# Stores to intermediate DRAM buffers issued by GpSimd in place of SyncE, in a two-layer encoder kernel

## The chip, the core and the metric

The kernel runs on one core of a Trainium2 chip. A core has TensorE (matmul, PE in the profile; PEld is its weight load), VectorE (DVE), ScalarE (ACT), GpSimd (POOL) and SyncE (SP). Each engine works through its own list of instructions in order and waits for the others on semaphores. A DMA is issued by an engine (SP, ScalarE or GpSimd) from its list, and 16 DMA engines move the bytes. The metric is the device time of one execution in microseconds (us).

## The reference

Two layers work on x of 2048 tokens with 1024 features, float32.

```python
def even_layer(x, ...):
    h = rmsnorm(x, norm_pre)
    xa, za, xb, gb, gc, zb = split(h @ w_in)               # 1024 x 6144
    ua = centred_dwconv(xa, conv_w, 2) + conv_b
    ya = rg_lru(ua, ..., False) + rg_lru(ua, ..., True)    # scans over the tokens, both ways
    ya = ya * silu(za)
    yb = gb * centred_dwconv(gc * xb, sc_w, 1) * silu(zb)
    return x + rmsnorm(concat([ya, yb]) @ w_out, norm_post)

def odd_layer(x, ...):
    h = rmsnorm(x, norm_pre)
    q, k, v, r, lr = split(h @ w_in)                       # 512, 512, 1024, 1024, 32
    log_alpha = log_sigmoid(lr @ w_gate_lr + b_gate) / 16  # one for each direction
    o = gla(q, k, v, log_alpha[0]) + flip(gla(flip(q, k, v, log_alpha[1])))
    o = rmsnorm(o, head_norm_g)                            # per head, 4 heads
    return x + rmsnorm((o * silu(r)) @ w_out, norm_post)
```

## The kernel before

All matrices are held as pairs of float16 (a high and a low part), and a product is three matmuls: high x high, high x low, low x high. The large products use a scheme of seven block products in place of eight (`quad`, `seven`, `wq_seven`), so each operand and each weight exists as seven sums or differences of blocks. These do not all fit on the chip. They are written to buffers in DRAM and read back when their block comes. The buffers, as the profile names them:

- hd, written from H by `op_save` (line 580): the seven operands of the even layer's input product, for two halves of the tokens x; read back by `op_loader` 107 times (H<-hd).
- yd, from YH by `yfin` (962): the 16 rows of blocks of the even mixer's result; read back as YC.
- x (x1 in the source), from XR by `post_even` (1249): the even layer's result.
- gd, from H by `op2_save` (1306): the seven operands of the odd layer; read back 56 times (H<-gd).
- wdqk, wdv, wdr, from hl by `save_u` in `w_prep` (1399): the odd layer's weights in seven sums for q and k, v, r; wzd the small gate weight. wqd, from PC and hl by `save_q` (1442): the odd layer's output weights.
- vd, rd, gld, yod: v (`v_save`), the gate r (`r_out`), the decays (`decays`) and the odd mixer's result (`y_out`).

The kernel is written as some fifty Python generators ("threads"), each for one strand of the work. The class `Order` runs them at build time. Each step of a thread announces an engine and an estimated cost, and the planner picks the step that can start first by its own clock. The instruction is put into its engine's list at that moment. On the chip each engine follows its list in order. A DMA counts as engine "D" in the plan: `dma` (line 282) announces bytes / 360e3 us and issues on SP. So SP's list holds loads and stores mixed, in the order of the plan, and an instruction of SP that waits holds up all behind it: a store waits until its data are computed, a load until its buffer is free.

Buffers on the chip come from pools: 23 large slots with a limit for each role (H, YL, H2, ...), the weight slots raw (3 or more), and hl, which during `w_prep` serves as small pieces. `w_prep` runs while TensorE does the even layer's output product (lines 1176 to 1178, `wo_mm`). For each pair of weight blocks, `prep` (1449) takes a piece for a running sum, makes seven results (high part on ScalarE, line 255; low part on VectorE, line 259; sums on VectorE, line 263) and stores each one; a piece is given back after its store (`pput`). In the same time `post_even` evacuates the product, normalises it and makes the odd layer's operands; the sum over features is a product with ones, split in two parts (`ones_mm2`, hv, line 463).

A wdv buffer has 256 columns, and each store fills 128 of them:

```python
def save(j, p):
    d = wu_d[u, j]
    yield from dma(d[:, :, :, i * 128:i * 128 + 128] if u[0] == "v" else d, p.t, 256 * 1024)
    pput(p)
```

GpSimd's own work before the change is two masks at the start (`consts`) and two memsets in `wz_load` (lines 1508 and 1509), which wait for the end of the even layer's output product.

Of the kernel before, what the change touches and what calls it, by code (L numbers as in the profile page):

```python
# [8 lines left out]
F16 = mybir.dt.float16  # L9
# [153 lines left out]
def trunk_kernel(ctx: ExitStack, tc: tile.TileContext, xT, w_in, gate_w, w_out, odd_w, lr_w, lr_gw, odd_wo, params, outT):  # L163
    nc = tc.nc
# [114 lines left out]
        yield from stt(out, v, 3.0 / scale, out, ALU.subtract, ALU.mult)  # L279
        unbank(b)  # L280

    def dma(out, in_, nbytes):
        yield ("D", nbytes / 360e3)
        nc.sync.dma_start(out=out, in_=in_)

    def done(ev):
        ev.t = S.cur.ready
# [287 lines left out]
    OPS = {}  # L575
    evOp = {}
    h_d = [[drams.tile([128, 4, 2, CH], F16, tag=f"h{x}{j}", name=f"hd{x}{j}") for j in range(7)] for x in range(2)]
    evHd = [[Ev() for _ in range(7)] for _ in range(2)]

    def op_save(x, j):  # L580
        yield ("w", evOp[x, j])
        yield from dma(h_d[x][j], OPS[x, j].t, 2 ** 20)
        done(evHd[x][j])
        if x == 0:
            if j in (0, 2, 4):
                yield ("w", ev_plain)
            put(OPS[x, j])
# [370 lines left out]
    y_d = [drams.tile([128, 2, T], F16, tag=f"y{i}", name=f"yd{i}") for i in range(16)]  # L958
# [3 lines left out]
    def yfin(ki, y):  # L962
        yh = yield from get("YH", [128, T])
        yield from act(yh.t, y.t, AF.Square, accum=ssq[:, ki:ki + 1])
        yield ("V", 0.35)
        e = sex[:, ki:ki + 1]
        nc.vector.tensor_scalar(out=e, in0=ssq[:, ki:ki + 1].bitcast(I32), scalar1=24, scalar2=None,
                                op0=ALU.arith_shift_right)
        nc.vector.tensor_scalar(out=sY[:, ki:ki + 1], in0=e, scalar1=-1, scalar2=202, op0=ALU.mult, op1=ALU.add)
        nc.vector.tensor_scalar(out=sW[:, ki:ki + 1], in0=e, scalar1=1, scalar2=65, op0=ALU.mult, op1=ALU.add)  # L970
        nc.vector.tensor_scalar(out=sY[:, ki:ki + 1], in0=sY[:, ki:ki + 1], scalar1=23, scalar2=None,
                                op0=ALU.arith_shift_left)
        nc.vector.tensor_scalar(out=sW[:, ki:ki + 1], in0=sW[:, ki:ki + 1], scalar1=23, scalar2=None,
                                op0=ALU.arith_shift_left)
        done(evS[ki])
        yv = yh.t.bitcast(F16)
        hi, lo = yv[:, 0:T], yv[:, T:2 * T]
        yield from act(hi, y.t, AF.Copy, scale=sYf[:, ki:ki + 1])
        yield from stt(lo, y.t, sYf[:, ki:ki + 1], hi, ALU.mult, ALU.subtract)
        put(y)  # L980
        yield from dma(y_d[ki].rearrange("p a t -> p (a t)"), yv, 2 ** 20)
        put(yh)
        done(evY[ki])

# [233 lines left out]
    x1_d = [[drams.tile([128, 4, CH], F32, tag=f"x1{c}{h}", name=f"x1{c}{h}") for h in range(2)] for c in range(NCH)]  # L1218
# [30 lines left out]
    def post_even():  # L1249
        yield ("w", ev_proj)  # L1250
        for c in range(NCH):
            if c == 0:
                yb = []
                for _ in range(2):
                    s = yield from get("YB", [128, 4, CH])
                    yb.append(s)
            tmp = yield from wget("hv", [128, 2, CH], F32)
            yield from evac_norm({m: _LazyOB(OB, c, m) for m in range(8)}, [evO[c, m] for m in range(8)], yb, tmp, 1, 2.0 ** -13, gsc[:, 0:8])
            b = yield from ones_mm2("fg", tmp.t[:, 0], late=4.0 if c < 3 else 0.0)
            r = tmp.t[:, 1]  # L1260
            yield from rsq(r, b, 1.0 / 1024, 0)
            for hf in range(2):
                yield ("w", evXR[c, hf])
                x, y = XR[c, hf].t, yb[hf].t
                yield from tt(y, y, r[:, None, :].to_broadcast([128, 4, CH]), ALU.mult)
                yield from tt(x, x, y, ALU.add)
                yield from act(y, x, AF.Square)
                yield from dma(x1_d[c][hf], x, 2 ** 20)
                if hf:
                    done(evX1[c])  # L1270
            yield from tt(yb[0].t, yb[0].t, yb[1].t, ALU.add)
            y = yb[0].t
            yield from tt(y[:, 0:2], y[:, 0:2], y[:, 2:4], ALU.add)
            yield from tt(y[:, 0], y[:, 0], y[:, 1], ALU.add)
            b = yield from ones_mm2("fg", y[:, 0], late=4.0 if c < 3 else 0.0)
            yield from rsq(r, b, 1.0 / (1024 * 4096), 1)
            if c == NCH - 1:
                for s in yb:
                    put(s)
            for hf in range(2):  # L1280
                x = XR[c, hf].t
                for k in range(4):
                    yield from stt(x[:, k], x[:, k], gsc[:, 16 + hf * 4 + k:17 + hf * 4 + k], r, ALU.mult, ALU.mult)
                if c % 2 == 0:
                    S.spawn(op2_make(c // 2, 2 * hf, XR[c, hf]), 1)
            if c % 2:
                S.spawn(op2_rest(c // 2), 1)
            wput(tmp)
            done(evH2[c])

    class _LazyOB:
# [3 lines left out]
        t = property(lambda s: s.d[s.k].t)  # L1295
# [5 lines left out]
    OP2 = {}  # L1301
    evOp2 = {(x, j): Ev() for x in range(2) for j in range(7)}
    h2_d = [[drams.tile([128, 4, 2, CH], F16, tag=f"g{x}{j}", name=f"gd{x}{j}") for j in range(7)] for x in range(2)]
    evH2d = [[Ev() for _ in range(7)] for _ in range(2)]

    def op2_save(x, j):
        yield from dma(h2_d[x][j], OP2[x, j].t, 2 ** 20)
        done(evH2d[x][j])

    def op2_make(x, j, src):  # L1310
# [58 lines left out]
    wq_d = [drams.tile([128, 4, 2, 512], F16, tag=f"wq{j}", name=f"wqd{j}") for j in range(8)]  # L1369
# [25 lines left out]
    wz_d = drams.tile([128, 2, 512], F16, tag="wzd", name="wzd")  # L1395
# [3 lines left out]
    def w_prep():  # L1399
        yield ("w", ev_proj)  # L1400
        w = W["lr", 0]
        yield ("w", w.evr)
        for hf in range(2):
            p = yield from pget()
            LRP.append(p)
            src = w.raw.t[:, hf * 4:hf * 4 + 4]
            yield from act(p.t[:, 0], src, AF.Copy, scale=1024.0)

            lo = p.t[:, 1, :, 96:128]
            yield from stt(lo, src[:, :, 96:128], 1024.0, p.t[:, 0, :, 96:128], ALU.mult, ALU.subtract)  # L1410
            yield from act(p.t[:, 0, :, 96:128], lo, AF.Copy)
        wput(w.raw)
        done(evLRP)
        def save_u(u, i, last):
            def save(j, p):
                d = wu_d[u, j]
                yield from dma(d[:, :, :, i * 128:i * 128 + 128] if u[0] == "v" else d, p.t, 256 * 1024)
                pput(p)
                if last:
                    done(evWD[u, j])  # L1420
            return save

        for u in UNITS:
            prs = ukeys(u)
            for i, pr in enumerate(prs):
                yield from prep(W[pr[0]], W[pr[1]], save_u(u, i, i == len(prs) - 1))
            if u == UNITS[0]:
                w = W["wz", 0]
                p = yield from pget()
                wz = p.t.rearrange("p a k m -> p a (k m)")  # L1430
                yield ("w", w.evr)
                raw = w.raw.t.rearrange("p k m -> p (k m)").rearrange("p (d n) -> p d n", d=2)
                yield from act(wz, raw, AF.Copy, scale=256.0)
                yield from stt(wz[32:64], raw[32:64], 256.0, wz[32:64], ALU.mult, ALU.subtract)
                wput(w.raw)
                yield from dma(wz_d, wz, 256 * 1024)
                pput(p)
                done(evWZd)

        done(evPrep)  # L1440

    def save_q(hd):
        def save(j, p):
            yield from dma(wq_d[j][:, hd], p.t.rearrange("p a k m -> p a (k m)"), 256 * 1024)
            pput(p)
            count(("wq", j), 4, lambda: done(evWQd[j]))
        return save
# [192 lines left out]
    V = [[None, None] for _ in range(4)]  # L1640
    evVd = [Ev() for _ in range(4)]
    v_d = [[drams.tile([128, 8, 256], F32, tag=f"v{h}{x}", name=f"vd{h}{x}") for x in range(2)] for h in range(4)]
# [17 lines left out]
                         wfin, ofin)  # L1660

    def v_save(h, x):
        yield from dma(v_d[h][x], V[h][x].t, 2 ** 20)
        put(V[h][x])
        done(evVs[h][x])

# [26 lines left out]

    def r_out(h, x, s):
        yield from act(s.t, s.t, AF.Silu)
        yield from dma(r_d[h][x], s.t.rearrange("p a i t -> p a (i t)"), 2 ** 20)
        put(s)
        done(evRd[h][x])

# [68 lines left out]
    def decays(d):  # L1768
# [4 lines left out]
        for hd in range(4):  # L1773
# [35 lines left out]
                rng = crt[:, 1:16]  # L1809
            put(t1)  # L1810
            yield from act(rng, rng, AF.Exp, scale=-1.0 / 16)
            yield from dma(g_d[hd, d], t2.t, 2 ** 20)
            put(t2)
            done(evGd[hd, d])
        count("decays", 2, lambda: put(LMS[0]))
# [235 lines left out]

    def y_out(hd, c, yl):
        n = yn(c)
        yield from dma(yo_d[hd][c][:, 0:n], yl.t.bitcast(F16)[:, 0:n], 256 * n)
        put(yl)
        done(evYO[hd, c])

# [367 lines left out]
```

## Time and profile before

| | |
|---|---|
| median of 3 runs | 2169.05 us (2167.36 to 2171.09) |
| the profiled execution | 2169.87 us, its span 2168.0 us |
| TensorE busy | 2128.0 us (98%) |
| VectorE, ScalarE busy | 1579.9 us (73%), 1266.2 us (58%) |
| GpSimd busy | 2.8 us, 8 instructions |
| DMA | 458.36 MB, mean 211 GB/s; queue q1 took 57.2% of the 16 engines' span |
| granted TensorE clock | 0.997 |

The span runs from the first to the last instruction of the profiled execution. In rows of the timeline the first two numbers are the start and the duration in us, then the engine, the line of the source, the operation, what it writes and reads (by the program's names, numbers left out), the shape, and in brackets how long the engine stood idle before it and what ended the wait. SPq is SP's queue: a row there is the issue of a DMA, not its transfer. Rows of waits give who waited, for whom, and the total, the number of times and the longest in us. Rows of DMA issues end with the median time from issue to landing. Rows of stretches give for each engine its busy time, then the granted clock, the busy share of the DMA engines and GB/s.

### The profile page before, as it was taken

To read this page: it belongs to the slowest core of one execution; us is meant where nothing else is said; L and a number is where in the kernel's file an instruction comes from. 1 tells how busy PE (TensorE), PEld (TensorE's weight loads), DVE (VectorE), ACT (ScalarE), POOL (GpSimd) and SP (SyncE) were. 2 spreads that over 40 slices of the span, in tenths; PEclk is the share of its full clock that TensorE was granted. 3 is DMA by queue.
4 is the path that set the end of the run, shared out by engine and by line. 5 is a ranking of instruction groups with operands and counts; after the bars stand their busy time and mean duration, and the time that the engine had idled before them with its cause. 6 is when DMAs were issued, how large, how long until landed. Compare 5 with 4: busy or idle time off the path is not lost.

```text
span 2168.0 us, 28942 instructions
## 1 busy us (share of the span) xinstructions
PE 2128.0 (98%) x11650; PEld 1196.4 (55%) x11650; DVE 1579.9 (73%) x1908; ACT 1266.2 (58%) x1701; POOL 2.8 (0%) x8
## 2 busy tenths in 40 slices
PE   8999999999999999999999999999999999999997
PEld 5444444444444444444444444777657484858886
DVE  6998878887879787867467875676535748485866
ACT  5466877768677667765434443366446556466522
POOL 0000000000000000000000000000000000000000
PEclk9999999999999999999999999999999999999999
DMA  7165444555736555549767684147672939576353
GB/s 263 64 252 224 153 182 162 211 195 190 261 137 221 221 190 211 197 152 341 241 190 241 233 293 184 77 170 297 248 291 103 358 124 349 199 301 270 141 189 133
DMA packets 146150, 458.36 MB, mean 211 GB/s; under 512 B 39776, under 2 KB 60384, under 8 KB 111840
## 3 DMA queue, kind: packets, MB, share of 16 engines
q1 hardware_dynamic: 146016, 456.52, 57.2%
q8 instruction: 91, 1.49, 0.3%
q14 instruction: 43, 0.35, 0.1%
HBM read 329.99 MB, written 126.48 MB: 211 GB/s over the span
## 4 chain that ended last, share of the span: by engine, by line
PE 82%; DVE 8%; DMA 5%; ACT 3%; issue 2%; SPq 1%; ACTq 0%; DVEq 0%
PE ps L840 16%; PE ps L842 16%; PE ps L841 15%; PE ps L1178 3%; PE ps L1176 3%; PE ps L1177 3%; PE ps L1919 2%; PE ps L2154 2%; PE ps L2155 2%; PE ps L2156 2%; PE ps L1584 2%; PE ps L1586 2%; PE ps L1585 2%; PE ps L926 2%; PE ps L1887 1%
## 5 line engine op out<-in xcount | busy, mean ns | idle before, releaser
L840 PE MATMUL ps<-H,hl 128*128 128x512 f16 x848 | 322.3, 380 | 6.2 <-ACT QS L255 3.0
L841 PE MATMUL ps<-H,hl 128*128 128x512 f16 x848 | 322.1, 380 | 0.7 <-DVE H L263 0.7
L842 PE MATMUL ps<-H,hl 128*128 128x512 f16 x848 | 322.0, 380 | 0.2
L842 PE MATMUL ps<-H,PC 128*128 128x512 f16 x728 | 275.9, 379 | 1.0 <-DVE PC L259 1.0
L840 PE MATMUL ps<-H,PC 128*128 128x512 f16 x728 | 275.9, 379 | 0.8 <-DMA H<-hd 0.8
L841 PE MATMUL ps<-H,PC 128*128 128x512 f16 x728 | 275.9, 379 | 0.0
L1178 PE MATMUL ps<-YC,WO 128*128 128x512 f16 x512 | 194.1, 379 | 0.3 <-DVE WO L259 0.3
L1176 PE MATMUL ps<-YC,WO 128*128 128x512 f16 x512 | 194.1, 379 | 0.0
L1177 PE MATMUL ps<-YC,WO 128*128 128x512 f16 x512 | 194.0, 379 | 0.0
L840 PEld LDWEIGHTS <-hl 128*128 128x128 f16 x848 | 83.1, 98 | 103.9 <-issue 3.1
L842 PEld LDWEIGHTS <-hl 128*128 128x128 f16 x848 | 83.1, 98 | 102.3 <-issue 1.9
L841 PEld LDWEIGHTS <-hl 128*128 128x128 f16 x848 | 83.2, 98 | 101.4 <-issue 4.8
L1584 PE MATMUL ps<-WV,H 128*128 128x256 f16 x448 | 122.1, 273 | 1.8 <-ACT VD L255 1.8
L1585 PE MATMUL ps<-WV,H 128*128 128x256 f16 x448 | 122.1, 273 | 0.0
L1586 PE MATMUL ps<-WV,H 128*128 128x256 f16 x448 | 122.1, 273 | 0.0
L255 ACT ACTIVATE hl<-raw 128x512 f16<-128x512 f32 (+1 forms) x129 | 80.0, 629 | 69.2 <-DMA wdv<-hl 16.6
L842 PEld LDWEIGHTS <-PC 128*128 128x128 f16 x728 | 71.2, 98 | 87.2 <-DVE PC L259 1.5
L840 PEld LDWEIGHTS <-PC 128*128 128x128 f16 x728 | 71.2, 98 | 87.1 <-DMA H<-hd 1.3
L841 PEld LDWEIGHTS <-PC 128*128 128x128 f16 x728 | 71.2, 98 | 86.0 <-issue 0.3
L259 DVE SCALAR_TENSOR_TENSOR hl<-raw,hl 128x512 f16<-128x512 f32 (+2 forms) x129 | 87.4, 685 | 42.8 <-ACT hl L255 42.6
L155 ACT ACT_TABLE_LOAD x86 | 110.3, 1283 | 1.5
L263 DVE TENSOR_TENSOR SB<-ps,SB 128x256 f32<-128x256 f32 x112 | 46.4, 423 | 79.7 <-PE ps L1919 78.1
(252 smaller groups left out, 4523.2 us busy)
## 6 DMA issues: line engine op xcount, KB each, us to landing
H<-hd SPq DMA_DIRECT2D x107, 1024.0 KB, 6.2
H<-gd SPq DMA_DIRECT2D x56, 1024.0 KB, 10.3
raw<-w_in SPq DMA_DIRECT2D x48, 512.0 KB, 4.3
yd<-YH SPq DMA_DIRECT2D x16, 1024.0 KB, 4.9
YC<-yd SPq DMA_DIRECT2D x64, 256.0 KB, 5.0
hd<-H SPq DMA_DIRECT2D x14, 1024.0 KB, 4.8
gd<-H SPq DMA_DIRECT2D x14, 1024.0 KB, 4.2
raw<-odd_w SPq DMA_DIRECT2D x24, 512.0 KB, 5.6
```

Of the source, the lines that this page charges most:

```text
L155: self.load(SETS[self.table][0])
L255: nc.scalar.activation(out=out, in_=in_, func=func, scale=scale, **kw)
L259: nc.vector.scalar_tensor_tensor(out=out, in0=in0, scalar=scalar, in1=in1, op0=op0, op1=op1)
L840: nc.tensor.matmul(b.t[:, sl], lhsT=wh, rhs=hi, start=s, stop=False, skip_group_check=True)
L841: nc.tensor.matmul(b.t[:, sl], lhsT=wh, rhs=lo, start=False, stop=False, skip_group_check=True)
L842: nc.tensor.matmul(b.t[:, sl], lhsT=wl, rhs=hi, start=False, stop=e, skip_group_check=True)
L1176: nc.tensor.matmul(b.t, lhsT=wh, rhs=hi, start=start, stop=False)
L1177: nc.tensor.matmul(b.t, lhsT=wh, rhs=lo, start=False, stop=False)
L1178: nc.tensor.matmul(b.t, lhsT=wl, rhs=hi, start=False, stop=stop)
L1584: nc.tensor.matmul(b.t[:, i], lhsT=hi, rhs=wh, start=st, stop=False, skip_group_check=True)
L1585: nc.tensor.matmul(b.t[:, i], lhsT=hi, rhs=wl, start=False, stop=False, skip_group_check=True)
L1586: nc.tensor.matmul(b.t[:, i], lhsT=lo, rhs=wh, start=False, stop=e, skip_group_check=True)
```

## The change

The helper for DMAs gets an argument for the issuing engine, and 13 stores of the source pass GpSimd: all that write an intermediate buffer. In the program 203 of SP's 696 instructions move to GpSimd's list: 14 hd, 16 yd, 8 x, 14 gd, 84 wdqk, wdv and wdr, 1 wzd, 32 wqd, 6 vd, 8 rd, 8 gld and 12 yod. The loads and the ten stores of the output stay on SP. The announced cost in the plan is unchanged, and so the lists of TensorE, VectorE and ScalarE hold the same rows in the same order. On GpSimd the stores stand in the order of the plan.

```diff
-    def dma(out, in_, nbytes):
+    def dma(out, in_, nbytes, eng=nc.sync):
         yield ("D", nbytes / 360e3)
-        nc.sync.dma_start(out=out, in_=in_)
+        eng.dma_start(out=out, in_=in_)
...
     def op_save(x, j):
         yield ("w", evOp[x, j])
-        yield from dma(h_d[x][j], OPS[x, j].t, 2 ** 20)
+        yield from dma(h_d[x][j], OPS[x, j].t, 2 ** 20, eng=nc.gpsimd)
...
-        yield from dma(y_d[ki].rearrange("p a t -> p (a t)"), yv, 2 ** 20)
+        yield from dma(y_d[ki].rearrange("p a t -> p (a t)"), yv, 2 ** 20, eng=nc.gpsimd)
...
     def op2_save(x, j):
-        yield from dma(h2_d[x][j], OP2[x, j].t, 2 ** 20)
+        yield from dma(h2_d[x][j], OP2[x, j].t, 2 ** 20, eng=nc.gpsimd)
...
-                yield from dma(d[:, :, :, i * 128:i * 128 + 128] if u[0] == "v" else d, p.t, 256 * 1024)
+                yield from dma(d[:, :, :, i * 128:i * 128 + 128] if u[0] == "v" else d, p.t, 256 * 1024, eng=nc.gpsimd)
                 pput(p)
...
     def y_out(hd, c, yl):
         n = yn(c)
-        yield from dma(yo_d[hd][c][:, 0:n], yl.t.bitcast(F16)[:, 0:n], 256 * n)
+        yield from dma(yo_d[hd][c][:, 0:n], yl.t.bitcast(F16)[:, 0:n], 256 * n, eng=nc.gpsimd)
```

The same edit stands at the stores of x1_d, wz_d, wq_d, v_d, r_d and g_d.

Three places in the lists, each with the names used above (the numbers tell one tile or buffer from another; 1024x1x128 is 1024 rows of 128 numbers).

SP's list in `w_prep`, where the wdv stores begin, as the difference between before (-) and after; raw is a weight slot, hl a piece:

```order
 L284 DMA raw_7668<-odd_w 128x1024
-L284 DMA wzd<-hl_7278 128x1024
-L284 DMA wdqk_150<-hl_7278 128x1024
-L284 DMA wdv_153<-hl_7281 1024x1x128
-L284 DMA wdv_155<-hl_7278 1024x1x128
-L284 DMA wdv_154<-hl_7278 1024x1x128
-L284 DMA wdv_158<-hl_7281 1024x1x128
-L284 DMA wdv_159<-hl_7278 1024x1x128
-L284 DMA wdv_156<-hl_7278 1024x1x128
 L284 DMA raw_7776<-odd_w 128x1024
```

The load of the next weight block stood behind eight stores and now follows the load before it. GpSimd's list of after holds the same stores:

```order
 L284 DMA wzd<-hl_7278 128x1024
 L284 DMA wdqk_150<-hl_7278 128x1024
 L284 DMA wdv_153<-hl_7281 1024x1x128
 L284 DMA wdv_155<-hl_7278 1024x1x128
 L284 DMA wdv_154<-hl_7278 1024x1x128
 L284 DMA wdv_158<-hl_7281 1024x1x128
 L284 DMA wdv_159<-hl_7278 1024x1x128
 L284 DMA wdv_156<-hl_7278 1024x1x128
```

They keep their order among themselves, with no load between them. SP's list at the end of the even layer, where the last results are stored (yd) while operands (hd) and output weights (w_out) are loaded, difference as above:

```order
 L284 DMA raw_7180<-w_out 128x1024
 L284 DMA H_7157<-hd_91 128x4096
-L284 DMA yd_114<-YH_7105 128x4096
 L284 DMA H_7199<-hd_92 128x4096
 L284 DMA raw_7214<-w_out 128x1024
```

The operand load H_7199 no longer has a store before it. SP's list in the odd layer, where the first results of a head are stored (yod) and operands (gd) and the gate (rd) loaded:

```order
 L284 DMA H_1070_12595<-gd_133 128x4096
 L284 DMA H_1072_12615<-gd_134 128x4096
-L284 DMA yod_251<-YL_12356 128x3584
 L284 DMA YL_12742<-rd_226 128x2x512
 L284 DMA H_1074_12638<-gd_135 128x4096
```

The store that stood between the operand loads is gone from this list; the gate's load stays between them.

More of the change, by code (lines that the diff above doesn't have):

```diff
@@ L1267, in post_even @@
                 yield from act(y, x, AF.Square)
-                yield from dma(x1_d[c][hf], x, 2 ** 20)
+                yield from dma(x1_d[c][hf], x, 2 ** 20, eng=nc.gpsimd)
                 if hf:
@@ L1435, in w_prep @@
                 wput(w.raw)
-                yield from dma(wz_d, wz, 256 * 1024)
+                yield from dma(wz_d, wz, 256 * 1024, eng=nc.gpsimd)
                 pput(p)
@@ L1443, in save @@
         def save(j, p):
-            yield from dma(wq_d[j][:, hd], p.t.rearrange("p a k m -> p a (k m)"), 256 * 1024)
+            yield from dma(wq_d[j][:, hd], p.t.rearrange("p a k m -> p a (k m)"), 256 * 1024, eng=nc.gpsimd)
             pput(p)
@@ L1662, in v_save @@
     def v_save(h, x):
-        yield from dma(v_d[h][x], V[h][x].t, 2 ** 20)
+        yield from dma(v_d[h][x], V[h][x].t, 2 ** 20, eng=nc.gpsimd)
         put(V[h][x])
@@ L1695, in r_out @@
         yield from act(s.t, s.t, AF.Silu)
-        yield from dma(r_d[h][x], s.t.rearrange("p a i t -> p a (i t)"), 2 ** 20)
+        yield from dma(r_d[h][x], s.t.rearrange("p a i t -> p a (i t)"), 2 ** 20, eng=nc.gpsimd)
         put(s)
@@ L1811, in decays @@
             yield from act(rng, rng, AF.Exp, scale=-1.0 / 16)
-            yield from dma(g_d[hd, d], t2.t, 2 ** 20)
+            yield from dma(g_d[hd, d], t2.t, 2 ** 20, eng=nc.gpsimd)
             put(t2)
```

## Prediction

> **What bounds the kernel now.** I read the top of the page first, then TensorE's waits, then the same waits by place.
>
> ```profile
> span 2168.0 us, 28942 instructions
> PE 2128.0 (98%) x11650; PEld 1196.4 (55%) x11650; DVE 1579.9 (73%) x1908; ACT 1266.2 (58%) x1701; POOL 2.8 (0%) x8
> 0.00:50.00 50.00, 42.71 (x145) 28.81 (x146) 32.52 (x66) 23.76 (x30) 0.79 (x6) 1.00 0.81 285
> 2150.00:2168.00 18.00, 5.90 (x50) 4.71 (x48) 7.38 (x10) 3.14 (x8) 0.00 (x0) 0.78 0.17 59
> ```
>
> TensorE is busy for 2128.0 of 2168.0 us, so 40.0 us are idle in the whole program. The two stretches (second number: TensorE's busy time) hold 7.3 us of that at the start and 12.1 us at the end. Neither depends on a store to an intermediate buffer: the first waits for inputs, the last for the final block. The most that any change of the middle can win is therefore 40.0 - 7.3 - 12.1 = 20.6 us, and it wins only what TensorE waits for there because of a transfer.
>
> ```profile
> PE ps L840 <- DMA H<-gd: 3.8, 2, 3.6
> PE ps L840 <- ACT QS L255: 3.0, 1, 3.0
> PE ps L840 <- DMA H<-hd: 2.4, 2, 1.7
> PE ps L463 <- DVE hv L263: 1.9, 2, 1.4
> ```
>
> Of TensorE's waits (total, times, longest) two rows are transfers in the middle, 3.8 + 2.4 = 6.2 us. The rest are ScalarE and VectorE. POOL, with 2.8 us of work, has room for 203 stores. So the change is small on the winning side; what it can lose has to be looked for where an engine waits for a store to land.
>
> **What the change takes away: loads that stand behind a store.** SP runs its queue in order. Here is its queue at the two places where TensorE waits longest for a load, and TensorE's own rows.
>
> ```profile
> 990.54 0.38 SPq L284 DMA_DIRECT2D H<-hd  x1
> 993.07 0.32 SPq L284 DMA_DIRECT2D yd<-YH  x1
> 993.49 0.38 SPq L284 DMA_DIRECT2D H<-hd  x1
> 1001.72 0.39 PE L840 MATMUL ps<-H,hl 128*128 128x512 f16 x1 [1.67 <-DMA H<-hd]
> 1680.44 3.20 SPq L284 DMA_DIRECT2D H<-gd  x4
> 1698.53 0.32 SPq L284 DMA_DIRECT2D yod<-YL  x1
> 1698.94 0.52 SPq L284 DMA_DIRECT2D YL<-rd  x1
> 1699.52 2.43 SPq L284 DMA_DIRECT2D H<-gd  x3
> 1707.89 0.38 PE L840 MATMUL ps<-H,raw 128*128 128x512 f16 x1 [3.59 <-DMA H<-gd]
> ```
>
> At 993 the operand load H<-hd follows the store yd<-YH by 0.42 us (993.49 - 993.07); SP had stood at that store since about 990.9. Without it the load can start up to 2.5 us earlier, more than the 1.67 us that TensorE waits. At 1698 SP stood at the store yod<-YL from 1683.6 (1680.44 + 3.20) to 1698.53, and three H<-gd loads behind it started at 1699.52. If the buffer is free, the first starts up to 15 us earlier and the 3.59 us go. I take both in full: -1.67 - 3.59 = -5.3 us. The bounds are 0 (the buffer itself is late) and -6.2 us (both DMA rows).
>
> **What it puts in their place.** A store is now made by POOL. No DMA of POOL is in this trace, so its price is bounded from rows.
>
> ```profile
> L284 SPq DMA_DIRECT2D wdv<-hl x28: 512/522/2749, 1069.1 to 1139.8; - x28
> L284 SPq DMA_DIRECT2D wdr<-hl x28: 319/320/988, 1147.5 to 1302.7; - x28
> 1.13 0.34 POOL L324 TENSOR_SCALAR_AFFINE_SELECT ident<-ones 128x128 f32<-128x128 f32 x1 [0.63 <-DVE ones L319]
> 1337.22 1.80 POOL L1508 MEMSET LM<- 128x2048 uint8 x1 [1335.51 <-PE ps L1178]
> ```
>
> The first two rows are SP's issue times (min/median/max in ns, first and last start). A store of 128 rows costs SP 0.32 us, a wdv store 0.52. A wdv store is 1024 rows of 256 bytes, because it writes half of each row of its buffer. The lower bound on POOL is SP's own price, 0.32 and 0.52 us. For the upper bound I take POOL's longest instruction, 1.80 us, per 128 rows: 1.80 and 8 x 1.80 = 14.4 us. The value that I take is the shorter of POOL's two kinds of work, 0.34 us per 128 rows, since it lies nearest to SP's 0.32: 0.34 us for a store of 128 rows and 8 x 0.34 = 2.7 us for a wdv store, if the rows are written one by one.
>
> The Trainium skill (DMA: Bandwidth & Descriptors, "SWDGE vs HWDGE vs iDMA") says that a GpSimd DMA has its descriptors written by software on GpSimd, where SP's come from dedicated hardware, and "Latency and other measured facts" gives the first byte after about 1 us against 0.6. By that alone each store would land 0.4 us later, an estimate of 28 / 3 x 0.4 = 4 us over the wdv stores in place of the 13 below; no run so far shows it.
>
> Who waits for a store to land? Only the weight preparation (prep), between 1040 and 1345 us:
>
> ```profile
> DVE hl L263 <- DMA raw<-odd_w: 35.6, 9, 6.3
> ACT hl L255 <- DMA wdv<-hl: 34.2, 19, 9.9
> ACT hl L255 <- DMA wdr<-hl: 18.9, 9, 8.1
> ACT hl L255 <- DMA wdqk<-hl: 15.8, 8, 6.4
> wdqk<-hl SPq DMA_DIRECT2D x28, 256.0 KB, 2.2
> wdv<-hl SPq DMA_DIRECT2D x28, 256.0 KB, 3.7
> ```
>
> Four pieces of hl go round, one for a sum and three for results; ScalarE cannot write the next result before the store of the third last has landed (median 3.7 us for wdv, last column). ScalarE and VectorE run in order too, and behind these copies stand the square, the copy and the sum that the normalisation needs. TensorE waits for the end of that:
>
> ```profile
> 1146.93 0.49 PE L463 MATMUL ps<-hv,ones_r 128*128 128x512 f32 x1 [1.44 <-DVE hv L263]
> 1218.45 0.68 DVE L263 TENSOR_TENSOR hv<-YB,hv 128x512 fp32r<-128x512 f32 x1
> 1220.09 0.82 PE L463 MATMUL ps<-hv,ones_r 128*128 128x512 f32 x2
> 1311.18 0.69 DVE L263 TENSOR_TENSOR hv<-YB,hv 128x512 fp32r<-128x512 f32 x1 [0.70 <-ACT hv L255]
> 1319.48 0.82 PE L463 MATMUL ps<-hv,ones_r 128*128 128x512 f32 x2
> ```
>
> This is the heart of it. At 1146.93 TensorE already waits 1.44 us for VectorE: there is no slack, and all that the wdv stores lose before that point reaches TensorE one for one. At 1220 the slack is 1.0 us (1220.09 - 1219.13), at 1319 it is 7.6.
>
> The wdv stores run from 1069.1 to 1139.8: 70.7 us. On POOL, in order, 28 x 2.7 = 76 us. POOL also stands idle while a new pair of weights is awaited: mean 35.6 / 9 = 4.0 us, three times between these stores, 12 us, of which I take half, 6, since POOL then still works off one or two stores. The last store lands 2.7 - 0.5 = 2.2 us later. So 76 + 6 + 2.2 - 70.7 = +13 us, and TensorE has no cover for it. At the lower bound (0.52) it is 0; at the upper, 14.4 x 28 - 70.7 = +332.
>
> The 56 stores wdqk and wdr of 128 rows come 2.8 us apart on average ((1302.7 - 1147.5) / 56), above even the 1.80 bound, so POOL keeps up. At 0.34 they add nothing. At 1.80 a landing is 1.5 us later, and eight pairs with 7 / 3 rounds each would make 28 us, less the slack of 1.0 and 7.6. I take 0.
>
> All other stores (hd, yd, x, gd, vd, rd, gld, yod, wqd, wzd) together: no row of TensorE names one, and their readers come later; 0, with one exception as bound. At 1044.03 TensorE waits 0.26 us at the end of a chain from the last yd store over the YC loads to a w_out load, and a later landing of that store adds up to 1.5 us. The two memsets of POOL keep their place, between gd and x stores after 1337; nothing behind them is awaited soon.
>
> The loads keep their order among themselves (the lists in the section on the change), so the first load of a new pair of weights now waits for its own slot only; in the stretch above that shortens the 4.0 us waits by an amount that I leave to the rivals.
>
> **The sum.** -5.3 + 13 + 0 + 0 = +7.7 us. The profiled execution took 2169.87 us, which gives 2177.6; it lies 0.8 above the median of the runs, 2169.05, so against that 2176.8: I say 2177. The price at which the two sides cancel is p with 28p + 6 + (p - 0.5) - 70.7 = 5.3, p = 2.4 us per wdv store; everything hangs on that one unknown.
>
> **The rivals.**
> - *Loads win.* POOL's price is well under 2.4 us, and the preparation gains as well, since the weight loads no longer wait behind stores: then -5.3 and the 1.44 us at 1146.93, 2169.05 - 6.7 = 2162. For it: SP's own price grows only from 0.32 to 0.52 with eight times the rows. Against it: TensorE can gain nothing more than its waits.
> - *No change.* The price is near 2.4, or buffers, not stores, hold the two loads and POOL is quick: 2169, within 4 us. For it: 98% busy.
> - *POOL is the bound.* At twice my price, 5.4 us, POOL works without a gap: 28 x 5.4 = 151, less 70.7, plus 4.9 for the last landing, less 5.3: +80, 2249. From 3.5 us on (28 x 3.5 + 6 + 3 - 70.7 - 5.3 = +31, 2200) I count the case as this one. For it: POOL's memset at 1.80 us is slow work; against it: stores of few rows are cheap on SP.
> - *VectorE holds POOL up.* If a store could not be written while VectorE works, each wdv store would wait for the end of an operation, 0.69 us for 512 elements: 28 x 0.69 = 19 more, 2196. VectorE's rows speak against it: 512 elements in 0.68 us is about one element at a time, nothing doubled. The Trainium skill (SBUF — State Buffer, "Who interferes with whom") says that GpSimd is locked out by VectorE's two-port modes, that tensor_tensor has none, and that descriptor writing needs only the write side; the trace agrees as far as those durations go.
>
> **How the numbers follow.** About 0.2%, 4.3 us, is what a measurement of this kernel tells from no change. Forecast (price 2.4 to 3.5; 2169 to 2200): 0.35. Loads win: 0.24. No change: 0.20. POOL is the bound: 0.16. VectorE holds POOL up: 0.05. Faster is 0.24; same is 0.20 and the lowest 0.04 of the forecast; slower is 0.31 + 0.16 + 0.05 = 0.52. The forecast's own range is 2169 to 2200. The range for all reaches from 2161 (loads win with everything) to 2250 (twice the price), leaving out the dearer half of POOL's case and a little below.
>
> **What would show it.** Right: 28 wdv stores on POOL's queue some 2.7 us apart, ScalarE's wait for wdv above 34.2 us, and TensorE's wait at the ones product (line 463) near 15 us in place of 1.9; the H<-gd and H<-hd waits of TensorE near zero. Wrong: a wdv store that costs POOL under 2 us with the wait at line 463 gone (loads win), or H<-gd still waiting 3.6 us although no store stands before it (the buffer was the cause).

## The result and the profile after

| | before | after |
|---|---|---|
| median of the runs | 2168.28 us (4 runs) | 2201.70 us (4 runs, 2199.97 to 2203.38) |
| ratio of after to before | | 1.0145, 95% interval 1.0132 to 1.0158 |
| span of the profiled execution | 2168.0 us | 2201.2 us |

The change costs about 33 us, where 8 were forecast. The top of the page after:

```profile
span 2201.2 us, 29068 instructions
PE 2133.9 (97%) x11650; PEld 1197.4 (54%) x11650; DVE 1580.5 (72%) x1908; ACT 1268.2 (58%) x1701; POOL 121.0 (5%) x211
```

GpSimd (POOL) is busy for 121 us of 2201, so it looks far from a limit. TensorE's idle time rose from 40.0 to 67.3 us (2201.2 - 2133.9), and its busy time by 5.9 us for the same 11650 products. TensorE's rows of waits (total, times, longest):

```profile
PE ps L463 <- ACT hv L255: 27.3, 3, 15.3
PE ps L840 <- DMA H<-hd: 4.4, 3, 2.0
PE ps L463 <- DVE hv L263: 1.2, 2, 0.8
PE ps L840 <- DMA H<-gd: 0.3, 1, 0.3
```

The product with ones (line 463) waits for 27.3 + 1.2 us, 26.6 more than the 1.9 before. H<-gd fell by 3.5, as forecast. H<-hd, forecast to go, rose from 2.4 to 4.4. The timeline shows the two long waits during the weight preparation:

```profile
1114.07 1.60 PE L463 MATMUL ps<-hv,ones_r 128*128 128x512 f32 x2 [11.56 <-ACT hv L255]
1179.32 1.52 PE L463 MATMUL ps<-hv,ones_r 128*128 128x512 f32 x2 [15.30 <-ACT hv L255]
```

Both stand after the start of the wdv stores. The rows of the wdv stores, then ScalarE's wait for them, and the median landings of after:

```profile
L284 POOL DMA_DIRECT2D wdv<-hl x28: 847/856/878, 1073.3 to 1178.3; - x28
  issue: 62.9, 21
ACT hl L255 <- DMA wdv<-hl: 70.6, 23, 5.6
wdv<-hl POOLq DMA_DIRECT2D x28, 256.0 KB, 3.3
wdqk<-hl POOLq DMA_DIRECT2D x28, 256.0 KB, 4.4
wdr<-hl POOLq DMA_DIRECT2D x28, 256.0 KB, 3.7
```

The 28 stores now take 105.0 us from first to last start, before 70.7. One costs POOL 0.86 us of work. The second row is the odd one: before 21 of them POOL stood idle, 62.9 us in all, and what ended the idle time is "issue", that is, no data and no other engine that the profile shows. POOL's timeline in the middle of that stretch:

```profile
1102.49 0.85 POOL L284 DMA_DIRECT2D wdv<-hl  x1 [2.65 <-issue]
1105.92 0.86 POOL L284 DMA_DIRECT2D wdv<-hl  x1 [2.58 <-issue]
1109.36 0.85 POOL L284 DMA_DIRECT2D wdv<-hl  x1 [2.58 <-DVE raw L263]
1185.62 0.54 POOL L284 DMA_DIRECT2D wdr<-hl  x1 [3.35 <-DVE hl L259]
```

Most of the wdv stores start about 3.44 us apart (1109.36 - 1105.92), and no two start closer than 3.43: 0.86 of work and 2.58 of waiting for something that no row names. (At 1109.36 the same 2.58 us stand under VectorE's name, so the name says little there.) With the pauses between pairs of weights the mean distance is 3.9 us (105.0 / 27). The 3.44 us are about one landing (3.3 us, row above): each store seems to wait until the one before has landed. The wdr stores of 128 rows, behind them, cost 0.54 us and wait almost only for VectorE.

TensorE's own work there, by stretches (second number: its busy time; the granted clock stands behind POOL), and two of its rows behind the first long wait:

```profile
1100.00:1150.00 50.00, 38.42 (x166) 16.85 (x165) 19.25 (x26) 13.03 (x20) 11.91 (x14) 0.86 0.47 119
1150.00:1200.00 50.00, 34.70 (x150) 15.29 (x149) 34.09 (x41) 17.22 (x21) 10.36 (x15) 0.83 0.59 189
1116.34 0.63 PE L1178 MATMUL ps<-YC,WO 128*128 128x512 f16 x1
1119.17 0.38 PE L1176 MATMUL ps<-YC,WO 128*128 128x512 f16 x1
```

In these stretches the granted clock is 0.86 and 0.83; before it was 1.00 in both. Behind each of the two long waits a product takes 0.63 us in place of 0.38, for about 5 us (the granted clock is 0.50 from 1116 to 1118 us), and from then on 0.38 again. The lines concerned (463 and 1176 to 1178) hold 5.4 of the 5.9 us of longer busy time. So the 33.2 us of span come apart into 26.6 (line 463), 5.9 (slower products), 2.0 (H<-hd) and -3.5 (H<-gd), with 2.2 left over for small rows.

### The profile page after: what moved, and what is told of

It is laid out like the page before. It is cut to its first block, busy times and chain, and to the rows that moved or that the text cites. A ratio compares the mean times of both kernels' runs of the same rounds, so it can differ in the third digit from the quotient of the medians.

```text
span 2201.2 us, 29068 instructions
## 1 busy us (share of the span) xinstructions
PE 2133.9 (97%) x11650; PEld 1197.4 (54%) x11650; DVE 1580.5 (72%) x1908; ACT 1268.2 (58%) x1701; POOL 121.0 (5%) x211
## 4 chain that ended last, share of the span: by engine, by line
PE 82%; issue 7%; DVE 5%; DMA 3%; ACT 3%; POOL 1%; SPq 0%; POOLq 0%; ACTq 0%; DVEq 0%
PE ps L842 16%; PE ps L840 16%; PE ps L841 16%; PE ps L1176 3%; PE ps L1177 3%; PE ps L1178 3%; PE ps L1919 2%; PE ps L2155 2%; PE ps L2154 2%; PE ps L2156 2%; PE ps L1584 2%; PE ps L1585 2%; PE ps L1586 2%; PE ps L1887 1%; PE ps L1963 1%
```

## The experiments

Two questions were open: what the 2.58 us are, and why the loads gained less than 5.3 us. A ratio compares a kernel's runs with those of before in the same batch; it need not be the quotient of the medians, which stand beside it.

### Which stores cost the time

The first run gives the wdv stores back to SP and leaves the other 175 on GpSimd.

```diff
-   p.t, 256 * 1024, eng=nc.gpsimd)
+   p.t, 256 * 1024, eng=nc.sync if u[0] == "v" else nc.gpsimd)
```

> The changed kernel with one store put back: the 28 wdv stores are issued by SP again, the other 175 stay on GpSimd. Theory W (the wdv stores carry the loss: 3.44 us apart on GpSimd, 27.3 us of TensorE's wait at line 463): the wait falls to 2 us or less and the time to 2165 to 2173. Rival G (any store costs more on GpSimd; the wdqk and wdr landings went from 2.2 and 2.1 to 4.4 and 3.7 us): 2180 to 2195, with ScalarE's waits for wdqk and wdr still above 40 us and a wait at line 463 of 10 us or more.

Measured: 2171.25 us beside 2171.16 for before, ratio 1.0002 (0.9991 to 1.0012). The second run is the reverse: the kernel before, with the wdv stores alone on GpSimd (the same line, `eng=nc.gpsimd if u[0] == "v" else nc.sync`).

> The kernel before with only the 28 wdv stores on GpSimd. Theory W: the whole loss is there, 2195 to 2206, wdv stores 3.4 us apart. Rival G: under 2185. The TensorE wait for H<-gd of 3.6 us is still there, since the yod stores stay on SP.

Measured: 2202.12 us, ratio 1.0142 (1.0125 to 1.0159). Its waits of TensorE and its wdv stores:

```profile
PE ps L463 <- ACT hv L255: 25.2, 2, 13.4
PE ps L840 <- DMA H<-gd: 3.9, 2, 3.4
L284 POOL DMA_DIRECT2D wdv<-hl x28: 851/852/987, 1074.1 to 1176.9; - x28
```

The whole loss stands in these 28 stores; the other 175 add nothing in sum. The H<-gd wait is still there, since yod is back on SP.

### What a wdv store waits for

GpSimd's DMAs use memory that the program reserves for their descriptors, 2048 bytes here. The Trainium skill (DMA: Bandwidth & Descriptors, "Terms") says that a descriptor has 16 bytes and that GpSimd's are written to rings in SBUF; "The descriptor swizzle" counts, for one transfer of 1 MiB to 128 partitions, 8 data descriptors and one for completion on each side of each of the 16 DMA engines. By that, as an estimate, 2048 bytes hold 128 pieces; a store of 128 rows takes 9 of them, and a wdv store of 1024 rows 65, so two wdv stores (130) do not fit. The runs test it from two sides. The first gives more memory and changes nothing else.

```diff
-dynamic_dma_scratch_size=2048
+dynamic_dma_scratch_size=2560
```

> The changed kernel with dynamic_dma_scratch_size 2560 in place of 2048, nothing else. Theory R (room): the memory reserved for GpSimd's DMAs holds one wdv store of 1024 rows but not two, so the next one waits until the one before is drained (2.58 us of idle after 0.86 us of work). 2560 bytes are 160 pieces of 16 bytes, two stores of 64 + 1 per DMA engine are 130: two fit, the spacing of most stores falls below 2.9 us and the time to 2165 to 2182. Rival P (price by rows: writing 1024 rows takes GpSimd 3.44 us, whatever is reserved): spacing 3.44 us, time 2199 to 2204. Rival L (the producers wait for landings, GpSimd is not the limit): also 3.44 us and no change.

```profile
L284 POOL DMA_DIRECT2D wdv<-hl x28: 847/847/983, 1073.0 to 1143.2; - x28
  issue: 16.7, 8
```

Measured: 2173.16 us, ratio 1.0009 (0.9999 to 1.0018). The work of a store is the same 0.85 us; the unnamed idle time falls from 62.9 to 16.7 us, and the stores take 70.2 us, as on SP (70.7). So the price was not work for each row. The second run gives as little more as it takes by the estimate: 2112 bytes, 132 pieces.

> The kernel after with the memory reserved for GpSimd's DMA descriptors at 2112 bytes in place of 2048, 132 pieces of 16 bytes in place of 128. Theory R (a store waits until its pieces have room; a wdv store of 1024 rows takes 65 of them, two take 130): two fit from 130 on, so 64 bytes are enough, the wdv stores come about 2.6 us apart as with 2560 bytes, the last one starts near 1143, and the time is near 2172. Rival R2 (the room matters gradually, or in larger steps): the pace stays near 3.44 us and the time near 2200.

```profile
L284 POOL DMA_DIRECT2D wdv<-hl x28: 844/853/962, 1069.5 to 1142.5; - x28
  issue: 23.6, 11
```

Measured in one run: 2168.44 us. 64 bytes bring the stores from 105.0 to 73.0 us and the time back to that of before (2170.51 in this batch); the last kernel below, also with 2112 bytes, has the same pace (1069.5 to 1141.8) and twelve runs at the time of before. The starts say more than the totals. Three of them with 2112 bytes:

```profile
1102.59 0.86 POOL L284 DMA_DIRECT2D wdv<-hl  x1 [1.04 <-DVE hl L259]
1104.49 0.85 POOL L284 DMA_DIRECT2D wdv<-hl  x1 [1.04 <-DVE hl L259]
1106.04 0.85 POOL L284 DMA_DIRECT2D wdv<-hl  x1 [0.71 <-DVE hl L259]
```

With 2048 bytes no store starts less than 3.43 us after the one before it. With 2112 and with 2560 bytes neighbours may follow at once, but no store starts less than 3.44 us after the second one before it (here 1106.04 - 1102.59 = 3.45). So one store at a time has room in the first case and two in the other two, and that is why 2560 bytes win nothing over 2112. Nor does GpSimd simply take one store at a time: in the kernel after, with 2048 bytes, a store of 128 rows (x<-XR at 1154.14) starts right behind a wdv store, as 65 + 9 pieces would by the estimate. The step lies between 128 and 132 pieces, where the estimate has it (130); that a store takes just 65 is not shown by itself.

From the other side: the memory stays at 2048 bytes, and the wdv buffers are laid out so that a store writes 128 whole rows.

```diff
-    drams.tile([128, 2, 4, 256 if u[0] == "v" else 128], ...)
+    drams.tile([128, 2, 2, 4, 128] if u[0] == "v" else [128, 2, 4, 128], ...)
...
-    dma(d[:, :, :, i * 128:i * 128 + 128] if u[0] == "v" else d, ...)
+    dma(d[:, i] if u[0] == "v" else d, ...)
...
-    wh, wl = wp[:, 0, k], wp[:, 1, k]
+    wh, wl = wp[:, :, 0, k], wp[:, :, 1, k]
```

> The changed kernel, with another layout of the wdv buffers: each store writes whole rows, 128 of 2048 bytes in place of 1024 of 256, and TensorE reads the weights as two halves of 128 columns in place of one of 256. Same bytes, same lists. Theories R and P: a store takes GpSimd 0.54 us as wdqk does, no idle behind it, time 2163 to 2172. Theory G: landings of 3.5 to 4.4 us still delay the pieces, 2175 to 2190. If TensorE reads two halves more slowly, its matmuls at lines 1584 to 1586 show it (273 ns before).

```profile
L284 POOL DMA_DIRECT2D wdv<-hl x28: 539/539/551, 1075.0 to 1137.2; - x28
  issue: 0.4, 2
```

Measured: 2169.29 us, ratio 0.9994 (0.9985 to 1.0004). The unnamed idle time is gone and a store costs 0.54 us, as the other stores of 128 rows do. The matmuls at lines 1584 to 1586 take 273 ns as before. To see what the layout does by itself, the same edit on before:

> The kernel before with whole-row wdv buffers, all stores on SP. It tells what the new layout is worth by itself. Both theories: a wdv store costs SP about 0.33 us in place of 0.52 and TensorE has one wait of 1.4 us there, so 0 to -1.5 us. If it gains more than 1.5 us, the equal time of the run with whole rows on GpSimd hid a loss of the same size elsewhere.

Measured: 2169.08 beside 2169.45 us, ratio 0.9991 (0.9981 to 1.0002): no difference that can be told, though the interval leaves room for a gain of up to 4 us. What whole rows win on GpSimd, the whole loss of 1.45%, is a matter of GpSimd's queue.

### Where the gain of the loads went

Without the loss at wdv, the kernels with the other stores on GpSimd come out level with before, though the H<-gd wait is gone from each of their profiles. So something gives it back. Three runs take the parts by themselves. First, before with yod alone on GpSimd:

> The kernel before, with the 12 yod stores alone on GpSimd. Theory S: the H<-gd loads no longer wait behind a yod store, TensorE's 3.6 us at H<-gd go, the time is 3 to 3.6 us under before. Rival N: the H<-gd wait goes and another takes its place; within 1 us of before.

Measured: 2168.42 beside 2169.45 us, ratio 0.9993 (0.9983 to 1.0002). TensorE's H<-gd wait is 0.5 us. The gain of 1.5 us (-3.7 to +0.4 as a change in time) settles neither theory. Second, before with only the even layer's stores (hd, yd, wqd) on GpSimd:

> The kernel before, with only the even layer's stores hd, yd and wqd on GpSimd. Theory S: TensorE waits for H<-hd go from 2.4 to about 4 us in three places, and the time is 1.5 to 4 us over before, with H<-gd still at 3.8. Rival N: within 1 us of before. The forecast of the prediction for this part (H<-hd gone) would be 1.7 us under before.

Measured: 2175.61 us, ratio 1.0024 (1.0013 to 1.0035), a loss of 5.2 us (0.0024 x 2169.45; 2.8 to 7.6), more than theory S had, with H<-hd at 4.2 us as it said. Third, the odd layer's stores on GpSimd, with whole-row wdv buffers, and the even layer's back on SP:

> The kernel after with whole-row wdv buffers, and the stores hd, yd and wqd of the even layer back on SP; the stores of the odd layer and of its weights stay on GpSimd. Theory S (two signs: the even layer's stores on GpSimd lose what the odd layer's win): H<-gd stays gone, H<-hd is back to about 2.4 us, and the time is 2 to 4 us under before, about 2167. Rival N (no net gain anywhere: what is won at H<-gd is waited out later): the time equals before within 1 us, about 2170, though the H<-gd row is gone.

Measured: 2167.16 us, ratio 0.9988 (0.9979 to 0.9997), the only kernel here that is faster than before by more than its interval, by 0.1%. It is one of a dozen comparisons, and whole rows by themselves gave 0.9991, so this gain cannot be put down to the odd layer's stores. The loss of the even layer's stores is clear of the noise; a gain of the odd layer's is not shown. Nor do the parts add up well: 5.2 - 2.6 would leave the kernel with whole rows and all stores on GpSimd 2.6 us over before, and it came out at 0.9994 (-3.3 to +0.9 us).

Where the profile shows the even layer losing: SP's and TensorE's rows of before, then POOL's, SP's and TensorE's of the kernel with the even part alone, with TensorE's wait for H<-hd in the whole program as the last row:

```profile
550.45 0.42 SPq L284 DMA_DIRECT2D wqd<-PC  x1
550.97 0.60 SPq L284 DMA_DIRECT2D H<-hd  x1
558.17 0.42 SPq L284 DMA_DIRECT2D wqd<-hl  x1
558.65 0.42 SPq L284 DMA_DIRECT2D wqd<-PC  x1
561.00 0.39 PE L840 MATMUL ps<-H,PC 128*128 128x512 f16 x1 [0.78 <-DMA H<-hd]
```

```profile
550.60 0.54 POOL L284 DMA_DIRECT2D wqd<-PC  x1
551.32 0.54 POOL L284 DMA_DIRECT2D wqd<-hl  x1 [0.18 <-issue]
551.85 0.54 POOL L284 DMA_DIRECT2D wqd<-PC  x1
551.81 1.26 SPq L284 DMA_DIRECT2D H<-hd  x1
554.22 1.85 SPq L284 DMA_DIRECT2D H<-hd  x1
562.25 0.39 PE L840 MATMUL ps<-H,hl 128*128 128x512 f16 x1 [2.04 <-DMA H<-hd]
566.02 0.39 PE L840 MATMUL ps<-H,PC 128*128 128x512 f16 x1 [1.00 <-DMA H<-hd]
PE ps L840 <- DMA H<-hd: 4.2, 3, 2.0
```

On SP two of the three wqd stores stood behind loads that waited for a buffer, and went out 7 us after the second H<-hd load (558.17 - 550.97). On GpSimd all three go out before it. No row of TensorE names these stores, but TensorE needs the load, and its waits grow from 0.78 to 3.04 us. This is so in every kernel here: with all of the even layer's stores on GpSimd (six kernels) the waits near 561 are 2.2 to 3.3 us in sum, with all of them on SP (six) 0.6 to 0.9. The queue of SP had kept urgent loads ahead of stores that nobody waits for, by accident of its order. SP's issue of the load also takes 1.85 us in place of 0.60; how much of the delay is issue and how much transfer the rows do not say.

Whether it is wqd or the others, the last two parts tell. Before with hd and yd alone, and before with wqd alone, on GpSimd:

> The kernel before with only the stores hd and yd on GpSimd; wqd stays on SP. Theory Q (what the even layer's stores lose comes from the wqd stores, which SP held back behind loads until 558 us and GpSimd sends at 549 to 552, in front of the H<-hd loads): TensorE's wait near 561 is back to about 0.8 us in one place, and the time is within 1.5 us of before. Rival Y (the yd and hd stores take the transfer from the loads): the waits near 561 stay at 3 us and the time 4 to 6 us over before, as with all three.

> The kernel before with only the 32 wqd stores on GpSimd. Theory Q: two waits near 561 of 3 us together in place of 0.8, and the time 2 to 5 us over before. Rival Y: one wait of 0.8 us there and the time within 1.5 us of before.

Measured: hd and yd 2173.08 beside 2170.51 us, ratio 1.0015 (1.0005 to 1.0024); wqd 2172.08, ratio 1.0007 (0.9997 to 1.0017). TensorE's rows near 561, the first of hd and yd, the others of wqd:

```profile
565.28 0.39 PE L840 MATMUL ps<-H,PC 128*128 128x512 f16 x1 [1.51 <-DMA H<-hd]
560.65 0.39 PE L840 MATMUL ps<-H,hl 128*128 128x512 f16 x1 [0.40 <-DMA H<-hd]
564.41 0.39 PE L840 MATMUL ps<-H,PC 128*128 128x512 f16 x1 [1.00 <-DMA H<-hd]
```

Neither theory holds alone. Each part has 1.4 to 1.5 us of waits here, more than the 0.78 of before, and less than the 3.04 of both; the losses in time (0.15% and 0.07%) add up to that of all three (0.24%) within the intervals. I had put all of it on wqd, which is wrong: hd and yd have as long a wait here. That a store on a queue of its own takes transfer from the loads beside it is a likely reason, but it is argued and not shown: in the kernel with hd and yd alone TensorE's waits for H<-hd are 2.5 us in all, as before (2.4), and its time is still longer. With all three the profiled waits for H<-hd explain 1.8 of the 5.2 us (4.2 against 2.4 in all); that profile is of an execution of 2171.55 us, 4 below the median of its runs. The rest stays open.

The last run puts the two findings together with the smallest edit: after, with the even layer's stores on SP and 2112 bytes.

> The kernel after with two edits that the runs so far point to: the even layer's stores hd, yd and wqd back on SP, and 2112 bytes for GpSimd's descriptors. The wdv buffers keep the old layout. Theory S with R: TensorE has no H<-gd wait of 3.6 us, H<-hd about 2.4 us as before, the hv product (line 463) waits under 3 us in all, and the time is 1.5 to 3.5 us under before, like the run with whole rows and the odd layer's stores. Rival N (that gain came from the whole rows): within 1 us of before.

Measured: 2170.84 beside 2171.52 us, ratio 0.9997 (0.9987 to 1.0007). H<-gd is gone from TensorE's waits, but the time is that of before within the interval, and the 1.5 to 3.5 us of theory S did not come. Of the gain of 0.1% seen with whole rows, 0.03% is left here, and the intervals overlap; whether the layout gives the rest was not settled. No gain here is larger than 0.1%.

## Why the prediction was wrong in size

- **The wdv stores: +13 forecast, 32.5 measured (26.6 of waits and 5.9 of clock).** The place, the waiting engines and the missing slack were right, but the delay came in two parts: 11.56 us already at the product that stood at 1097.81 before, where TensorE had not waited, and 15.30 at the one of 1146.93 that the forecast names. The step that failed is the price, "8 x 0.34 = 2.7 us for a wdv store": I priced a store by POOL's work for it. The work is 0.86 us; the pace was 3.44 because of 2.58 us of waiting for room in front of it. With 3.44 in the same formula, 28 x 3.44 + 6 + 2.9 - 70.7 = +34.5 us. That this comes near the 32.5 is in part luck: the pauses were 12 us and not 6 (105.0 - 27 x 3.44), and the 2.9 for a later landing did not come (median 3.7 us before, 3.3 after).
- **"Loads win".** By its work, 0.86 us, a store is well under the 2.4 of this rival, and the rival was right about work: eight times the rows cost 0.86 against 0.54. Its time did not come even without the wait: 2173.16 and 2169.29 beside 2171.16 for before.
- **The clock.** No term stood for it. Products took longer behind the two long waits (5.9 us in sum), and the run with wdv alone on GpSimd shows it too, 0.86 in both stretches; the kernels without the long waits at line 463 have 1.00 there.
- **"POOL is the bound", 2249 at twice the price, counted from 3.5 us on.** This rival had the size nearest (2200 at 3.5 us), and the wrong cause: POOL's queue was the bound while POOL was idle.
- **The loads: -5.3 forecast, -1.5 came in TensorE's waits (-3.5 and +2.0).** This is the second step that failed. With 3.44 in the formula and the loads as forecast the sum would have been 2169.05 - 5.3 + 34.5 = 2198; the 3.8 us that the loads did not win are about the rest. The two loads come next, one by one; the wait for H<-hd near 561, which grew from 0.78 to 3.03 us, stood in no term.
- **H<-gd: -3.59 forecast, 3.5 less wait.** The operand loads now precede the yod store:

```profile
1728.78 1.54 SPq L284 DMA_DIRECT2D H<-gd  x3
1733.52 0.53 POOL L284 DMA_DIRECT2D yod<-YL  x1 [19.18 <-DVE YL L259]
1739.34 0.38 PE L840 MATMUL ps<-H,raw 128*128 128x512 f16 x1 [0.32 <-DMA H<-gd]
```

  The wait fell as said. In time, the run with yod alone shows 1.5 us (ratio 0.9993; -3.7 to +0.4), which cannot be told from none.
- **H<-hd at 1001.72: -1.67 forecast, -0.28 came.** The load did start earlier, as said: 2.3 us ahead of the yd store (996.18 less about 993.9, where the second of the two begins), where it had stood 0.42 behind it. The rows of after, then the landings in the stretch from 985 to 1006 us, before and after:

```profile
993.38 0.86 SPq L284 DMA_DIRECT2D H<-hd  x2
996.18 0.53 POOL L284 DMA_DIRECT2D yd<-YH  x1 [79.46 <-DVE YH L259]
1004.27 0.39 PE L840 MATMUL ps<-H,hl 128*128 128x512 f16 x1 [1.39 <-DMA H<-hd]
```

```profile
H<-hd SPq DMA_DIRECT2D x2, 1024.0 KB, 7.2
yd<-YH SPq DMA_DIRECT2D x1, 1024.0 KB, 6.3
H<-hd SPq DMA_DIRECT2D x2, 1024.0 KB, 8.4
yd<-YH POOLq DMA_DIRECT2D x1, 1024.0 KB, 9.9
```

  Load and store both landed later, and the head start was eaten. With yd on GpSimd this wait is between 0 and 2.08 us in seven kernels, with yd on SP 1.55 to 1.69 in seven: it is shorter in six of the seven and gone in one. The Trainium skill (DMA: Bandwidth & Descriptors, "Queues, rings and completion order") says that a DMA engine takes packets from its queues in turn; the trace fits that, with 8.4 and 9.9 us in place of 7.2 and 6.3, but does not prove it: over the whole program the yd stores land later from GpSimd (median 7.1 in place of 4.9 us) and the H<-hd loads do not (5.9, before 6.2).
- **"All other stores ... 0".** Wrong for the even layer: 5.2 us when moved alone. "Their readers come later" was beside the point: near 561 TensorE waited longer for the loads that run beside the stores. The exception at 1044.03, a later yd store at the end of a chain, came as bounded: TensorE's waits for WO there rose from 0.26 to 1.88 us, most of the 2.2 left over above. The 56 wdqk and wdr stores were rightly taken at 0: TensorE waits at line 463 nowhere between 1181 and 1340, though their landings rose from 2.2 and 2.1 to 4.4 and 3.7 us. Their distance was misread: seven wdqk stores come before the wdv stores, so 49 stand in the stretch that was counted, 3.2 us apart and not 2.8; nothing hangs on it.
- **VectorE holds POOL up.** No sign of it: the 0.86 us of a store vary from 0.85 to 0.88, while VectorE works in a good part of the stretch, and with whole rows the unnamed idle time is gone (0.4 us).

## What to carry to other kernels

Before stores go to GpSimd, count the pieces of each (rows that are not contiguous) against the descriptor memory that the program reserves. In this kernel a store that took more than half of it could not overlap with the next, and the queue ran at the pace of landings while the engine looked idle. A little more of that memory, or a buffer laid out so that a store writes whole rows, cured it. A store that waits behind a load on a shared queue may be where it belongs: on a queue of its own it can go out ahead of loads that somebody waits for.

## What the runs showed of the hardware that was not expected

- A store from GpSimd costs 0.54 us of its time for 128 rows of 2048 bytes and 0.86 us for 1024 rows of 256 bytes; from SP 0.32 and 0.52 us.
- The start of a GpSimd store can wait 2.58 us for descriptor memory; the profile books this mostly as "issue" idle time (21 of 28 stores) and names no releaser. With 2048 bytes of it a store of 1024 rows started at the least 3.43 us after the one before; with 2112 and 2560 bytes this distance held for every second store. The mean distances were 3.9, 2.7 and 2.6 us.
- After waits of 11.56 and 15.30 us TensorE's products took 0.63 us in place of 0.38 for about 5 us; in the stretches of 50 us around them its granted clock was 0.86 and 0.83, where it had been 1.00.
